# The first loads of a hybrid flow-matching layer: which queue issues them, and in which order the first projection's weights and the adaLN slabs follow

## The chip, the cores and the metric

One core of one Trainium2 chip runs the whole program. The metric is device time in microseconds (us) of one execution, lower is better; the profile shows one execution instruction by instruction. In the program's names PE is the matrix engine, DVE the vector engine, ACT the scalar engine, POOL the GpSimd engine and SP the engine that issues most transfers.

## The reference, cut to what matters

All 384 tokens (128 of a context, 256 latents) pass one layer. Only its first part bears on the change:

```python
mod = silu(cond) @ ada_w + ada_b                  # 6 x 2048 values for each of two condition vectors
h = rmsnorm(x, norm_w[0]) * (1 + scale_a) + shift_a
q, k, v, o, g, u = split(h @ w_in)                # each of q k v o u: 2048 -> 1024; g: 2048 -> 32
hm = mlstm_bidirectional(q, k, v, gates(g)) ; hp = pool_mixer(u)
x = x + gate_a * rmsnorm(concat(hm, hp) @ w_out, norm_w[1])
x = x + gate_f * rmsnorm(relu(h2 @ w1) ** 2 @ w2, norm_w[3])
```

## The kernel before

**Precision.** Every weight tile is loaded in float32 ("raw"), ACT copies it to a rounded `hi`, DVE subtracts to get `lo`, and each product is three matmuls: `hh*hi`, `hl*hi`, `hh*lo`, where `hh` and `hl` are the same split of the activations. `load_w` does one such tile: a transfer issued on SP, the ACT copy, the DVE subtraction. The raw tiles share 3 buffers, `hi` and `lo` have 4 each.

**The opening.** ACT's queue issues the condition vectors `cc` (two transfers), the constants `cst`, and four transfers of parameters into `prm`; SP issues the three tiles of x (1 MB each, `xtok`), then eight slabs of `ada_w` (512 KB each, `ada_raw`), then the first two weight tiles of u. POOL issues the gate bias, `mprev` and `n_in`. PE transposes the parameters (`pp`), then x (`xt`), and multiplies the slabs with silu of the condition vectors (`ada`). From that come the first columns of `mod`, and `make_h` makes the first `hm`, `hh`, `hl`.

**The u and v stage.** A loop of 8 steps `s` takes 256 rows of the contraction each. In a step five chunks pass: `("u", 0)`, `("u", 512)`, `("v", 0)`, `("v", 3)`, `("v", 6)`; the last also holds the gate columns. Each chunk is one weight tile and, on PE, 18 matmuls. Between the chunks stand the pieces of the adaLN product for the next step, `next(ada0)`: in a later step eight slabs are loaded (three after chunk 0, three after chunk 1, two after chunk 2), then 64 matmuls after chunk 2, the small transposing matmuls in the middle of chunk 3, and after it `make_h(s + 1)`. Four of the eight slabs use free halves of the tiles `u` and the tile `masks`, four the tiles `ada_raw`. The results of a chunk are added to SBUF tiles `u`, `v`, `gsb` by DVE (by ACT in step 0).

**What sets the order.** PE's order is the order of the code. On SP, DVE, ACT and POOL a scheduler places the instructions of this stage. Every engine works its list off in order, an instruction that waits holds up all behind it. Transfers issued by SP and ACT share 8 completion semaphores (`DMAHW0` to `DMAHW7`) handed out in turn; a transfer that takes a semaphore again first waits for the one that had it before. POOL's transfers have semaphores of their own (`DMASW`).

After this stage come pooling and the mLSTM, the output projection, and the MLP with most of the time.

Of the kernel before, what the change touches and what calls it, by code (L numbers as in the profile page):

```python
# [13 lines left out]
P = 128  # L14
# [11 lines left out]
N_CST = 15  # L26
# [9 lines left out]
RATE_GS = 0.25  # L36
S_FIRST, S_LAST, N_LAST = 1, 6, 2
LAG = 4
RATES = (1.5, 1.3, 1.3)
GATE_AT = 1, 6, 10  # L40

# [2 lines left out]
def hymba_kernel(  # L44
# [6 lines left out]
    nc = tc.nc  # L51
# [13 lines left out]
    def bank(name):  # L65
        return psum.tile([P, 512], F32, tag="ps", name=name)


    cst = const.tile([P, 3, P], F32, name="cst")
    cs_src = consts.rearrange("p (n q) -> p n q", q=P)  # L70
    ident = cst[:, C_ID, :]
    ones = cst[:, C_ONE, :]
    cc = const.tile([P, 2, 16], F32, name="cc")
# [2 lines left out]
    pre = pre_scope.enter_context(tc.tile_pool(name="pre", bufs=1))  # L76
    prm = pre.tile([P, 2, P], F32, name="prm")
    masks = vp.tile([P, N_CST - 3, P], F32, name="masks")
    nc.scalar.dma_start(cc[:, 0, :], c_ctx.rearrange("(p j) -> p j", j=16))
    nc.scalar.dma_start(cc[:, 1, :], c[0].rearrange("(p j) -> p j", j=16))  # L80
    nc.scalar.dma_start(cst[:, 0:3], cs_src[:, 0:3])

    vsb = [vp.tile([P, NH, 129], F32, name=f"v{i}") for i in range(3)]
    gsb = vp.tile([P, 3, 32], F32, name="gsb")
    x_tok = [pre.tile([P, D], F32, tag=f"x{i}", name=f"xtok{i}") for i in range(3)]
    for t, src in zip(x_tok, (x_prompt[0], x_sample[0, 0:128], x_sample[0, 128:256])):
        nc.sync.dma_start(t, src)
    nc.scalar.dma_start(prm[0:96, 1, :], ada_b[0].rearrange("(r p) -> r p", p=P))
    nc.scalar.dma_start(prm[0:64, 0, :], norm_w[0].rearrange("i (k p) -> (i k) p", p=P))
    nc.scalar.dma_start(prm[64:72, 0, :], mlstm_norm_w[0].rearrange("(k p) -> k p", p=P))  # L90
    nc.scalar.dma_start(prm[72:80, 0, :], pool_scale[0].rearrange("(k p) -> k p", p=P))
    gbias = const.tile([P, 32], F32, name="gbias")
    nc.gpsimd.dma_start(gbias, gate_bias[0].rearrange("g h -> (g h)").partition_broadcast(P))
    mprev = const.tile([40, 3], F32, name="mprev")
# [27 lines left out]
    def load_w(pieces, name, n=1024, after=(), later=None):  # L122

        raw = wp.tile([P, 1024], F32, tag="raw", name=f"raw_{name}", bufs=3)
        a = pieces[0][1].shape[1]
        rv = raw[:, 0:n].rearrange("p (a b) -> p a b", a=a)
        for off, src in pieces:
            load_w.ins = nc.sync.dma_start(rv[:, :, off:off + src.shape[2]], src).ins
        hi = wp.tile([P, 1024], F32R, tag="hi", name=f"hi_{name}", bufs=N_W)
        lo = wp.tile([P, 1024], F32R, tag="lo", name=f"lo_{name}", bufs=N_W)  # L130
        with ExitStack() as es:
            for ins in after:
                es.enter_context(tc.issue_after(ins))
            nc.scalar.activation(hi[:, 0:n], raw[:, 0:n], AF.Copy)  # L134
            low = lambda: nc.vector.tensor_tensor(lo[:, 0:n], raw[:, 0:n], hi[:, 0:n].bitcast(F32), op=ALU.subtract)  # L135
            if later is None:
                low()
            else:
                later.append(low)
        return (hi[:, 0:n].rearrange("p (a b) -> p a b", a=a), lo[:, 0:n].rearrange("p (a b) -> p a b", a=a))  # L140
# [27 lines left out]
    def gemm_T(w, cols, xs, n, evac, feeds=(), korder=(0, 1, 2, 3), name="g", hold=None):  # L168
# [3 lines left out]
        for g, c0 in enumerate(cols):  # L172
            for o in range(2):
                acc[g, o] = bank(f"acc_{name}_{c0}_{o}")
        beside = hold or (lambda ki, g: steps_done[-LAG] if len(steps_done) >= LAG else ())
        for ki, kc in enumerate(korder):
# [165 lines left out]
    NS = len(ksteps)  # L342
# [91 lines left out]
    chunks = [("u", 0, 512), ("u", 512, 512), ("v", 0, 3), ("v", 3, 3), ("v", 6, 2)]  # L434
# [17 lines left out]
    def load_chunk(s, ci, after=(), later=None):  # L452
        kind, c0, w = chunks[ci]
        ks = slice(ksteps[s][0], sum(ksteps[s]))
        if kind == "u":
            n, pieces = w, [(0, wv_in[:, ks, U0 + c0:U0 + c0 + w])]
        else:
            n, pieces = w * P, [(0, wv_in[:, ks, V0 + c0 * P:V0 + (c0 + w) * P])]
            if c0 == 6:
                pieces.append((n, wv_in[:, ks, 4 * M:4 * M + 32]))  # L460
                n += 32
        return load_w(pieces, f"{kind}_{c0}_{s}", ksteps[s][1] * n, after, later) + (n,)

    lo_later = []
    w_first = load_chunk(0, 0, later=lo_later)

    def shift_rows():
        for _ in range(2):
# [5 lines left out]
    h_ins = make_h(0, shift_rows)  # L474
# [6 lines left out]
    for s in range(NS):  # L481
        for ci, (kind, c0, w) in enumerate(chunks):
            k0, nk = ksteps[s]
            hi, lo, n = w_first if s == 0 and ci < 2 else load_chunk(s, ci, h_ins if s == 0 else ())
            if s == NS - 1 and ci == 4:
                with tc.issue_after(load_w.ins):
                    nc.sync.dma_start(masks, cs_src[:, 3:N_CST])
            acc = [bank(f"{kind}_{c0}_{s}_{i}") for i in range(3)]

            ways = ((0, 0), (1, 0), (0, 1))  # L490
            for ps in [ways[n:n + 1] for n in range(3)] if s == ci == 0 else [ways]:
                for k in range(nk):
                    for i in range(3):
                        for a, b in ps:
                            nc.tensor.matmul(acc[i][:, 0:n], h[k0 + k][a][:, i * P:(i + 1) * P], (hi, lo)[b][:, k, :],  # L495
                                             start=k == 0 and a + b == 0, stop=k == nk - 1 and b == 1)
                    if ci == 3 and k == 0:
                        next(ada0, None)
            if s == ci == 0:
                w_first = load_chunk(0, 1, h_ins)  # L500
            if s == 0 and ci == XT_AT:
                while len(xT) < KT:
                    transpose_x(len(xT))
            for _ in range((ADA_STEPS if s == 0 else (1, 1, 1, 0, 0))[ci]):
                next(ada0, None)
            if ci == 3 and s < NS - 1:
                make_h(s + 1)
            for i in range(3):
                if kind == "u":
                    dst, src = u_sb[i][:, c0:c0 + w], acc[i][:, 0:n]  # L510
                else:
                    dst, src = vsb[i][:, c0:c0 + w, 0:128], acc[i][:, 0:w * P].rearrange("p (h e) -> p h e", e=P)
                if s == 0:
                    nc.scalar.activation(dst, src, AF.Copy)
                else:
                    nc.vector.tensor_tensor(dst, src, dst, op=ALU.add)
                if kind == "v" and c0 == 6:
                    nc.vector.tensor_tensor(gsb[:, i, :], acc[i][:, w * P:n], gbias if s == 0 else gsb[:, i, :], op=ALU.add)
# [267 lines left out]
    def mid_vec():  # L786
        for i, q in ((4, 0), (4, 1), (3, 0), (3, 1), (2, 0)):
            yield from ada_vec(i, 1024 * q, 1024)

    ada2 = Feed(mid_vec(), RATES[0])  # L790

# [31 lines left out]

    ada2.rate = RATES[1]
    mixs = [None] * KT
# [35 lines left out]
    for k in range(8):  # L861
        mixs[k] = split_T(mix[k][:, 0:NTOK], f"mx{k}")
    ada2.rate = RATES[2]
    mo = [None] * KT
# [24 lines left out]
    for cols in ([0, 256], [512], [768], [1024], [1280], [1536], [1792]):  # L889
        if cols[0] in (768, 1024, 1280):  # L890
            for m in range(2):
                n = len(early)
# [496 lines left out]
```

## Time and profile before

| | before |
|---|---|
| median of 3 runs | 1690.18 us (1689.3 to 1690.31) |
| the profiled execution's own time | 1689.57 us |
| its span from first to last instruction | 1687.9 us |
| PE busy | 1656.9 us, 98% of the span |
| DVE busy | 1340.3 us, 79% |
| ACT busy | 752.4 us, 45% |
| POOL busy | 130.9 us, 8% |
| moved by DMA | 320.95 MB, mean 190 GB/s |

A row of the timeline or of the chain gives the start and the duration in us, then the engine, the line of the code and the operation. `SPq` and `ACTq` are the issuing of transfers. A bracket at the end of a row tells how long the engine was idle before, and what ended that. A row by stretches gives the busy time of the engines, the granted clock, the busy share of the DMA engines and GB/s.

### The profile page before, as it was taken

The numbers are of one execution on the slowest core, as the hardware profiler recorded it, in microseconds if no ns is written. First come the engines' busy times: TensorE is split into PE (matmuls) and PEld (weight loads), VectorE is DVE, ScalarE is ACT, GpSimd is POOL, SyncE is SP. The second block draws the span as 40 slices with busy tenths as digits, with TensorE's granted clock in tenths as the row PEclk, the third lists the DMA queues.
The fourth block names the chain that finished last, engine by engine and source line by source line (L and its number), as shares of the span: only waits on it lengthen the run. The fifth ranks groups of instructions, "written<-read, shape, count | busy, mean of one in ns | idle before, by whom it ended". The sixth has DMA issues, their size and how long they took to land.

```text
span 1687.9 us, 27859 instructions
## 1 busy us (share of the span) xinstructions
PE 1656.9 (98%) x10965; PEld 1582.5 (94%) x10965; DVE 1340.3 (79%) x2009; ACT 752.4 (45%) x1225; POOL 130.9 (8%) x181
## 2 busy tenths in 40 slices
PE   6999999999999999999999999999999999999997
PEld 4888999999999989989999999999999999999996
DVE  3677769898999959997797688988588488588688
ACT  4332355555443345543444444444444444444443
POOL 0000002221000024430000000000000000000120
PEclk9999999999999999999999999999999999999999
DMA  9999857777789964754546245544344443433653
GB/s 319 316 296 298 277 160 256 238 250 223 237 270 309 311 203 129 217 153 126 173 152 194 88 138 173 158 150 140 110 150 127 124 138 114 149 122 112 187 183 134
DMA packets 258195, 320.95 MB, mean 190 GB/s; under 512 B 14752, under 2 KB 223248, under 8 KB 257680
## 3 DMA queue, kind: packets, MB, share of 16 engines
q1 hardware_dynamic: 250256, 303.41, 57.0%
q0 software_dynamic: 5856, 13.69, 2.8%
q10 hardware_dynamic: 1952, 2.07, 0.4%
q8 instruction: 86, 1.41, 0.3%
q14 instruction: 45, 0.37, 0.1%
HBM read 308.61 MB, written 10.51 MB: 189 GB/s over the span
## 4 chain that ended last, share of the span: by engine, by line
PE 90%; DVE 4%; DMA 3%; issue 1%; SPq 1%; ACT 0%; POOL 0%; DVEq 0%; ACTq 0%; POOLq 0%
PE acc_w L144 10%; PE acc_w L143 10%; PE acc_w L145 10%; PE y L1223 4%; PE y L1224 4%; PE y L1222 4%; PE v L495 4%; PE u L495 3%; PE acc_wo L143 3%; PE acc_wo L144 3%; PE acc_wo L145 3%; PE y_yz L1223 2%; PE y_yz L1222 2%; PE y_yz L1224 2%; PE y L1066 2%; PE y L1065 2%
## 5 line engine op out<-in xcount | busy, mean ns | idle before, releaser
L144 PE MATMUL acc_w<-h2l,hi_w 128*128 128x384 f32 (+1 forms) x1024 | 346.2, 338 | 0.5 <-DVE h2l L1016 0.5
L143 PE MATMUL acc_w<-h2h,hi_w 128*128 128x384 f32 (+1 forms) x1024 | 344.2, 338 | 1.2 <-ACT h2h L1012 1.2
L145 PE MATMUL acc_w<-h2h,lo_w 128*128 128x384 f32 (+1 forms) x1024 | 345.1, 337 | 0.0
L135 DVE TENSOR_TENSOR lo_w<-raw_w,hi_w 128x1024 fp32r<-128x1024 f32 x152 | 185.3, 1221 | 137.0 <-ACT hi_w L134 136.8
L134 ACT ACTIVATE hi_w<-raw_w 128x1024 fp32r<-128x1024 f32 x152 | 160.8, 1058 | 215.2 <-PE acc_w L144 94.9
L316 DVE SCALAR_TENSOR_TENSOR ada_acc<-ada_raw,sg,ada_acc 128x1024 f32<-128x1024 f32 (+1 forms) x240 | 252.0, 1080 | 0.8 <-DMA ada_raw<-in_ada_w_dram 0.7
L143 PEld LDWEIGHTS acc_w<-h2h,hi_w 128*128 128x128 f32 x1024 | 192.2, 188 | 2.8 <-ACT h2h L1012 2.0
L144 PEld LDWEIGHTS acc_w<-h2l,hi_w 128*128 128x128 f32 x1024 | 192.6, 188 | 1.2 <-DVE h2l L1016 0.8
L145 PEld LDWEIGHTS acc_w<-h2h,lo_w 128*128 128x128 f32 x1024 | 192.4, 188 | 0.3 <-DVE lo_w L135 0.2
L1208 ACT ACTIVATE hi_t<-w 128x1024 fp32r<-128x1024 f32 x104 | 109.6, 1060 | 119.1 <-DVE w L1244 34.3
L1209 DVE TENSOR_TENSOR lo_t<-w,hi_t 128x1024 fp32r<-128x1024 f32 x104 | 126.3, 1220 | 15.1 <-ACT hi_t L1208 14.8
L1209 DVE TENSOR_TENSOR lo_b<-w,hi_b 128x1024 fp32r<-128x1024 f32 x78 | 95.3, 1221 | 41.9 <-ACT hi_b L1208 41.6
L1208 ACT ACTIVATE hi_b<-w 128x1024 fp32r<-128x1024 f32 x78 | 82.5, 1059 | 98.1 <-PE acc_w L144 66.7
L134 ACT ACTIVATE hi_wo<-raw_wo 128x1024 fp32r<-128x1024 f32 x32 | 34.0, 1064 | 80.6 <-DMA raw_wo<-in_w_out_dram 57.4
L942 ACT ACTIVATE z<-acc_w 128x384 f32<-128x384 f32 x54 | 26.3, 487 | 75.1 <-PE acc_w L145 75.1
L495 PE MATMUL v<-hi_v,hh 128*128 128x384 f32 (+1 forms) x144 | 48.0, 333 | 0.0
L134 ACT ACTIVATE hi_v<-raw_v 128x768 fp32r<-128x768 f32 (+1 forms) x24 | 19.0, 793 | 64.4 <-DMA raw_v<-in_w_in_dram 55.6
L495 PE MATMUL v<-lo_v,hh 128*128 128x384 f32 (+1 forms) x144 | 46.6, 324 | 1.0 <-DVE lo_v L135 1.0
L495 PE MATMUL v<-hi_v,hl 128*128 128x384 f32 (+1 forms) x144 | 46.5, 323 | 0.0
L135 DVE TENSOR_TENSOR lo_wo<-raw_wo,hi_wo 128x1024 fp32r<-128x1024 f32 x32 | 38.8, 1217 | 7.8 <-ACT hi_wo L134 7.0
L143 PE MATMUL acc_k<-hh,hi_k 128*128 128x384 f32 x128 | 44.2, 345 | 0.0
L143 PE MATMUL acc_o<-hh,hi_o 128*128 128x384 f32 x128 | 43.9, 343 | 0.0
(2264 smaller groups left out, 4549.0 us busy)
## 6 DMA issues: line engine op xcount, KB each, us to landing
raw_w<-in_w_dram SPq DMA_DIRECT2D x152, 512.0 KB, 4.2
ada_raw<-in_ada_w_dram SPq DMA_DIRECT2D x130, 512.0 KB, 4.7
w<-in_w_dram SPq DMA_DIRECT2D x104, 512.0 KB, 4.1
raw_wo<-in_w_out_dram SPq DMA_DIRECT2D x32, 512.0 KB, 5.1
u<-in_ada_w_dram SPq DMA_DIRECT2D x18, 512.0 KB, 6.6
raw_u<-in_w_in_dram SPq DMA_DIRECT2D x16, 512.0 KB, 7.0
raw_q<-in_w_in_dram SPq DMA_DIRECT2D x16, 512.0 KB, 4.8
raw_k<-in_w_in_dram SPq DMA_DIRECT2D x16, 512.0 KB, 4.9
```

What stands on the lines that cost most here:

```text
L134: nc.scalar.activation(hi[:, 0:n], raw[:, 0:n], AF.Copy)
L135: low = lambda: nc.vector.tensor_tensor(lo[:, 0:n], raw[:, 0:n], hi[:, 0:n].bitcast(F32), op=ALU.subtract)
L143: nc.tensor.matmul(ps, lh, rh, start=start, stop=False)
L144: nc.tensor.matmul(ps, lh, rl, start=False, stop=False)
L145: mm3.ins = nc.tensor.matmul(ps, ll, rh, start=False, stop=stop).ins
L316: nc.vector.scalar_tensor_tensor(acc[:, g, :], raw[:, a, :], cj, acc[:, g, :], op0=ALU.mult, op1=ALU.add)
L495: nc.tensor.matmul(acc[i][:, 0:n], h[k0 + k][a][:, i * P:(i + 1) * P], (hi, lo)[b][:, k, :], start=k == 0 and a + b == 0, stop=k == nk - 1 ...
L1208: nc.scalar.activation(hi, raw, AF.Copy)
L1209: nc.vector.tensor_tensor(lo, raw, hi.bitcast(F32), op=ALU.subtract)
L1222: nc.tensor.matmul(acc, xh, wh, start=start and j == 0, stop=False)
L1223: nc.tensor.matmul(acc, xh, wl, start=False, stop=False)
L1224: nc.tensor.matmul(acc, xl, wh, start=False, stop=stop and j == 3)
```

## The change

```diff
--- before.py
+++ after.py
@@ -36,6 +36,7 @@
 LAG = 4
+N_AHEAD = 3
 RATES = (1.5, 1.3, 1.3)
@@ -76,19 +77,19 @@
-    nc.scalar.dma_start(cc[:, 0, :], c_ctx.rearrange("(p j) -> p j", j=16))
-    nc.scalar.dma_start(cc[:, 1, :], c[0].rearrange("(p j) -> p j", j=16))
-    nc.scalar.dma_start(cst[:, 0:3], cs_src[:, 0:3])
+    nc.sync.dma_start(cc[:, 0, :], c_ctx.rearrange("(p j) -> p j", j=16))
+    nc.sync.dma_start(cc[:, 1, :], c[0].rearrange("(p j) -> p j", j=16))
+    nc.sync.dma_start(cst[:, 0:3], cs_src[:, 0:3])
...
     for t, src in zip(x_tok, (x_prompt[0], x_sample[0, 0:128], x_sample[0, 128:256])):
         nc.sync.dma_start(t, src)
-    nc.scalar.dma_start(prm[0:96, 1, :], ada_b[0].rearrange("(r p) -> r p", p=P))
-    nc.scalar.dma_start(prm[0:64, 0, :], norm_w[0].rearrange("i (k p) -> (i k) p", p=P))
-    nc.scalar.dma_start(prm[64:72, 0, :], mlstm_norm_w[0].rearrange("(k p) -> k p", p=P))
-    nc.scalar.dma_start(prm[72:80, 0, :], pool_scale[0].rearrange("(k p) -> k p", p=P))
+    nc.gpsimd.dma_start(prm[0:96, 1, :], ada_b[0].rearrange("(r p) -> r p", p=P))
+    nc.gpsimd.dma_start(prm[0:64, 0, :], norm_w[0].rearrange("i (k p) -> (i k) p", p=P))
+    nc.gpsimd.dma_start(prm[64:72, 0, :], mlstm_norm_w[0].rearrange("(k p) -> k p", p=P))
+    nc.gpsimd.dma_start(prm[72:80, 0, :], pool_scale[0].rearrange("(k p) -> k p", p=P))
@@ -462,7 +463,16 @@
-    w_first = load_chunk(0, 0, later=lo_later)
+    loaded = {0: load_chunk(0, 0, later=lo_later)}
+
+    def load_ahead(m, n):
+        for q in range(m, min(m + n, NS * len(chunks))):
+            if q not in loaded:
+                s, ci = divmod(q, len(chunks))
+                loaded[q] = load_chunk(s, ci, h_ins if s == 0 else ())
+                if q == NS * len(chunks) - 1:
+                    with tc.issue_after(load_w.ins):
+                        nc.sync.dma_start(masks, cs_src[:, 3:N_CST])
@@ -481,10 +491,8 @@
-            hi, lo, n = w_first if s == 0 and ci < 2 else load_chunk(s, ci, h_ins if s == 0 else ())
-            if s == NS - 1 and ci == 4:
-                with tc.issue_after(load_w.ins):
-                    nc.sync.dma_start(masks, cs_src[:, 3:N_CST])
+            load_ahead(5 * s + ci, 1 if s + ci == 0 else N_AHEAD)
+            hi, lo, n = loaded.pop(5 * s + ci)
@@ -497,7 +505,7 @@
             if s == ci == 0:
-                w_first = load_chunk(0, 1, h_ins)
+                load_ahead(1, 1)
```

The opening transfers change queues, and the loop asks for a chunk's weights two chunks before it uses them, ahead of the slabs that are asked for in between. PE's list stays as it was. POOL's list has the four parameter transfers more at its head, ACT's seven transfers fewer. On SP, DVE and ACT the order of this stage changes; behind it, it is the same.

The head of SP's list, before (`xtok` is x, `ada_raw` the first slabs; in brackets the semaphores that a transfer waits for):

```order
L87 DMA xtok_89<-in_x_prompt_dram 128x2048
L87 DMA xtok_90<-in_x_sample_dram 128x2048 [waits DMAHW0_49]
L87 DMA xtok_91<-in_x_sample_dram 128x2048 [waits DMAHW1_49]
L252 DMA ada_raw_0_0_146<-in_ada_w_dram 128x4x256 [waits DMAHW2_49]
L252 DMA ada_raw_0_4_158<-in_ada_w_dram 128x4x256 [waits DMAHW3_49]
L252 DMA ada_raw_0_8_170<-in_ada_w_dram 128x4x256 [waits DMAHW4_49]
```

The second tile of x waits for the semaphore of the first `cc` transfer, since ACT's seven and the first tile of x have used all eight. The same place in the list after the change:

```order
L80 DMA cc<-in_c_ctx_dram 128x16
L81 DMA cc<-in_c_dram 128x16
L82 DMA cst<-in_consts_dram 128x384
L88 DMA xtok_89<-in_x_prompt_dram 128x2048
L88 DMA xtok_90<-in_x_sample_dram 128x2048
L88 DMA xtok_91<-in_x_sample_dram 128x2048
L253 DMA ada_raw_0_0_146<-in_ada_w_dram 128x4x256
L253 DMA ada_raw_0_4_158<-in_ada_w_dram 128x4x256
L253 DMA ada_raw_0_8_170<-in_ada_w_dram 128x4x256 [waits DMAHW0_49]
```

Three small transfers now stand ahead of x, and the first wait stands at the third slab, five transfers later.

SP's list where step 1 is loaded, before (`raw_u_1` and `raw_v_1` are weights of step 1; `u`, `masks` and `ada_raw_4` are the eight slabs whose product is needed in step 1):

```order
L128 DMA raw_u_1_556<-in_w_in_dram 128x2x512
L365 DMA u_250<-in_ada_w_dram 128x4x256
L365 DMA u_251<-in_ada_w_dram 128x4x256
L365 DMA u_252<-in_ada_w_dram 128x4x256
L128 DMA raw_u_1_590<-in_w_in_dram 128x2x512
L365 DMA masks<-in_ada_w_dram 128x4x256
L365 DMA ada_raw_4_0_618<-in_ada_w_dram 128x4x256
L365 DMA ada_raw_4_4_620<-in_ada_w_dram 128x4x256
L128 DMA raw_v_1_625<-in_w_in_dram 128x2x384
L365 DMA ada_raw_4_8_652<-in_ada_w_dram 128x4x256
L365 DMA ada_raw_4_12_654<-in_ada_w_dram 128x4x256
L128 DMA raw_v_1_693<-in_w_in_dram 128x2x384
```

and after:

```order
L129 DMA raw_u_1_482<-in_w_in_dram 128x2x512
L129 DMA raw_u_1_535<-in_w_in_dram 128x2x512
L129 DMA raw_v_1_568<-in_w_in_dram 128x2x384
L366 DMA u_250<-in_ada_w_dram 128x4x256
L366 DMA u_251<-in_ada_w_dram 128x4x256
L366 DMA u_252<-in_ada_w_dram 128x4x256
L129 DMA raw_v_1_602<-in_w_in_dram 128x2x384
L366 DMA masks<-in_ada_w_dram 128x4x256
L366 DMA ada_raw_4_0_630<-in_ada_w_dram 128x4x256
L366 DMA ada_raw_4_4_632<-in_ada_w_dram 128x4x256
L129 DMA raw_v_1_637<-in_w_in_dram 128x2x256
```

The second u tile has moved ahead of three slabs, the first v tile ahead of six; the last two slabs now follow the last weight tile of the step.

DVE's list in step 1, before (`u<-u_1` adds a chunk's result, `lo` is the subtraction that makes a weight tile ready):

```order
L516 TENSOR_TENSOR u_250<-u_1_0_562,u_250 128x512
L135 TENSOR_TENSOR lo_u_1_593<-raw_u_1_590,hi_u_1_592 128x1024
L516 TENSOR_TENSOR u_251<-u_1_1_563,u_251 128x512
L516 TENSOR_TENSOR u_252<-u_1_2_564,u_252 128x512
L516 TENSOR_TENSOR u_250<-u_1_0_596,u_250 128x512
L516 TENSOR_TENSOR u_251<-u_1_1_597,u_251 128x512
L516 TENSOR_TENSOR u_252<-u_1_2_598,u_252 128x512
L135 TENSOR_TENSOR lo_v_1_628<-raw_v_1_625,hi_v_1_627 128x768
```

and after:

```order
L136 TENSOR_TENSOR lo_u_1_538<-raw_u_1_535,hi_u_1_537 128x1024
L449 SCALAR_TENSOR_TENSOR hl_521<-hm_519,mod,hh_520 128x256
L526 TENSOR_TENSOR gsb<-v_0_0_541,gbias 128x32
L526 TENSOR_TENSOR gsb<-v_0_1_542,gbias 128x32
L526 TENSOR_TENSOR gsb<-v_0_2_543,gbias 128x32
L136 TENSOR_TENSOR lo_v_1_571<-raw_v_1_568,hi_v_1_570 128x768
L524 TENSOR_TENSOR u_250<-u_1_0_574,u_250 128x512
L524 TENSOR_TENSOR u_251<-u_1_1_575,u_251 128x512
```

Both subtractions now stand ahead of the additions of the first u chunk.

ACT's list at the change from step 1 to step 2, before (`hi` rounds a weight tile, `hh` the next step's activations):

```order
L134 ACTIVATE hi_u_2_782<-raw_u_2_780 128x1024 [waits DMAHW6_49,DVE_49,PE_49]
L268 ACTIVATE ada_sb_4_688<-ada_583 128x256 [waits PE_49]
L447 ACTIVATE hh_726<-hm_725,mod 128x128 [waits DVE_49]
L447 ACTIVATE hh_726<-hm_725,mod 128x256 [waits DVE_49]
L447 ACTIVATE hh_731<-hm_730,mod 128x128 [waits DVE_49]
```

and after:

```order
L135 ACTIVATE hi_u_2_708<-raw_u_2_706 128x1024 [waits DVE_49,DMAHW2_49,PE_49,Activation_49]
L269 ACTIVATE ada_sb_4_701<-ada_595 128x256 [waits PE_49]
L135 ACTIVATE hi_u_2_761<-raw_u_2_759 128x1024 [waits DMAHW3_49,DVE_49]
L135 ACTIVATE hi_v_2_794<-raw_v_2_792 128x768 [waits DMAHW4_49,DVE_49,PE_49]
L448 ACTIVATE hh_739<-hm_738,mod 128x128 [waits DVE_49]
L448 ACTIVATE hh_739<-hm_738,mod 128x256 [waits DVE_49]
```

Two more roundings of weights, one of them waiting for PE and for a transfer, now stand ahead of the activations of the next step.

## The prediction

> **What bounds the kernel now.** I read the page first, then the chain of waits, then the waits of SP and PE, and last the DMA rates by short stretches in the opening. From the page:
>
> ```profile
> span 1687.9 us, 27859 instructions
> PE 1656.9 (98%) x10965; PEld 1582.5 (94%) x10965; DVE 1340.3 (79%) x2009; ACT 752.4 (45%) x1225; POOL 130.9 (8%) x181
> PE 90%; DVE 4%; DMA 3%; issue 1%; SPq 1%; ACT 0%; POOL 0%; DVEq 0%; ACTq 0%; POOLq 0%
> ```
>
> PE bounds the kernel. A gain can only be time in which PE stands still. The change touches the part up to the end of the u and v stage; behind it every engine's list is the same, so what PE gains by then should reach the end nearly whole. The chain of waits, in order of time (start, duration, what):
>
> ```profile
> 18.73 8.55 DMA raw_u<-in_w_in_dram
> ...
> 28.71 4.63 PE u L495 x18
> ...
> 52.21 2.79 PE u L495 x12
> 55.63 1.23 DVE lo_u L135
> ...
> 71.33 4.08 PE v L495 x27
> 75.41 8.38 PE u L495 x36
> ...
> 113.04 1.06 ACT hi_u L134
> ...
> 119.09 8.35 PE u L495 x36
> ...
> 140.36 8.34 PE u L495 x36
> ...
> 161.60 8.33 PE u L495 x36
> ...
> 182.85 8.36 PE u L495 x36
> ```
>
> The u rows from 52.21 on (the v row serves later) are the starts of steps 1, 2, 4, 5, 6 and 7. From step 4 to step 7 a step takes (182.85 - 119.09) / 3 = 21.25 us, and the chain is PE alone. Step 1 takes 75.41 - 52.21 = 23.20, which is 1.95 too many; steps 2 and 3 take 43.68 together, 1.18 too many. So there are three places to gain: the 28.7 us before the first u matmul, 1.95 in step 1, 1.18 in steps 2 and 3.
>
> **The opening.** SP's waits and the timeline:
>
> ```profile
> SPq L87 <- DMA cc<-in_c_ctx_dram: 4.8, 1, 4.8
> ...
> 0.80 0.42 ACTq L79 DMA_DIRECT2D cc<-in_c_ctx_dram  x1
> 0.81 0.38 SPq L87 DMA_DIRECT2D xtok<-in_x_prompt_dram  x1
> 6.01 0.81 SPq L87 DMA_DIRECT2D xtok<-in_x_sample_dram  x2
> 6.86 11.82 SPq L252 DMA_DIRECT2D ada_raw<-in_ada_w_dram  x8
> ...
> xtok<-in_x_prompt_dram SPq DMA_DIRECT2D x1, 1024.0 KB, 5.0
> ```
>
> SP stood 4.8 us until the first `cc` transfer had landed, only to take its semaphore again. The DMA rate by stretches of 1 us (last column GB/s) shows the price:
>
> ```profile
> 3.00:4.00 1.00, 0.00 (x0) 0.00 (x0) 0.00 (x0) 0.00 (x0) 0.71 (x5) 1.00 0.92 380
> 4.00:5.00 1.00, 0.00 (x0) 0.00 (x0) 0.00 (x0) 0.00 (x0) 0.00 (x0) 1.00 1.08 423
> 5.00:6.00 1.00, 0.00 (x0) 0.00 (x0) 0.00 (x0) 0.00 (x0) 0.00 (x0) 1.00 0.94 215
> 6.00:7.00 1.00, 0.00 (x0) 0.00 (x0) 0.04 (x1) 0.71 (x1) 0.00 (x0) 1.00 0.76 162
> 7.00:8.00 1.00, 0.39 (x1) 0.18 (x1) 0.31 (x2) 0.99 (x3) 0.00 (x0) 1.00 0.75 123
> 8.00:9.00 1.00, 0.58 (x2) 0.28 (x2) 0.90 (x6) 0.97 (x3) 0.00 (x0) 1.00 0.94 385
> ...
> 29.00:30.00 1.00, 1.00 (x5) 0.69 (x5) 0.95 (x4) 1.00 (x4) 0.00 (x0) 1.00 1.07 342
> ...
> 61.00:62.00 1.00, 0.53 (x2) 0.20 (x2) 1.00 (x2) 0.00 (x0) 0.00 (x0) 1.00 0.50 149
> ```
>
> From 8 us the DMA engines are full (the row at 29 us is one of many like it; the first deep dip behind it that matters is at 61 us, last row), and the first u matmul hangs on the landing of `raw_u` (the chain above), so the opening is bound by bytes. A transfer issued at 6.01 is at full rate at about 8.0, 1.9 us later. After the change x stands behind three small transfers. SP takes about 0.43 us for one (0.81 for two, and gaps), so x's first tile is issued at 0.81 + 3 * 0.43 = 2.1, not 0.81, and flows from 4.0. Its 1.05 MB (1024 KB) at 0.40 MB/us, between the rows at 3 and 4 us, take 2.6 us, to 6.6; for the constants and parameters among it I add 0.4. The second tile then flows from about 7.0 without a gap, where before it flowed from 8.0. I take 0.9 us. Bounds: 1.3 lost, if the dead stretch stays and only the three issues count; 1.7 won, if the whole shortfall of 5 to 8 us goes (3 * 390 - 500 = 670 KB at 390 GB/s) and the issues cost nothing.
>
> The Trainium skill ("DMA: Bandwidth & Descriptors", section "Issuing engines are not separate DMA queues") says that all issuing engines feed the same 16 DMA engines, and that issuing from several at once only saves issue time. By that the opening would lose the three issues, 1.3 us, instead of winning 0.9. No row here contradicts the sharing; but the SP row shows a wait of 4.8 us which that rule does not count, so I go by the row.
>
> The parameters on POOL cost nothing. A POOL issue and its landing:
>
> ```profile
> 1.33 0.70 POOL L93 DMA_DIRECT2D gbias<-in_gate_bias_dram  x1 [0.81 <-POOLq L1376]
> gbias<-in_gate_bias_dram POOLq DMA_DIRECT2D x1, 16.0 KB, 5.2
> ...
> 13.90 0.47 PE L402 MATMUL xt<-cst,xtok 128*128 128x128 f32 x1 [2.10 <-DMA xtok<-in_x_sample_dram]
> ```
>
> Four issues of 0.70 from 1.33 on end at 4.1; the last lands at 3.43 + 5.2 = 8.6. PE needs them for `pp`, then waits for x's third tile until 13.90 anyway: that is the cover, 5 us of it, and without it the cost would be some 0.3 us. `gbias`, `mprev`, `n_in` go out 2.8 us later and are used after 50 us. ACT, rid of seven issues, waits for `cc` as before. The masks' transfer in step 7 has until pooling, past 190 us; nothing.
>
> **Step 1.** What PE waited for, and the rows that made it late:
>
> ```profile
> PEld v L495 <- DVE lo_v L135: 1.3, 1, 1.3
> PEld u L495 <- DVE lo_u L135: 0.5, 1, 0.5
> ...
> 55.02 0.69 DVE L516 TENSOR_TENSOR u<-u,u 128x512 f32<-128x512 f32 x1 [2.01 <-PE u L495]
> ...
> 60.01 0.85 ACT L134 ACTIVATE hi_v<-raw_v 128x768 fp32r<-128x768 f32 x1 [5.38 <-DMA raw_v<-in_w_in_dram]
> 61.54 0.95 DVE L135 TENSOR_TENSOR lo_v<-raw_v,hi_v 128x768 fp32r<-128x768 f32 x1
> ...
> 65.61 3.59 PE ada L372 x64
> ```
>
> The second `lo_u` stood on DVE behind an addition that waited for PE, and `raw_v` landed at 60.0, with six slabs ahead of it in a full DMA. After the change these six come behind it: 3.1 MB, 9 us at 350 GB/s (an estimate from the row at 29 us), so it lands near 51, and its subtraction stands ahead of the additions. Both waits go. What is late next are the slabs for step 1, but the bytes up to the last of them are the same that flowed by 61 us before; less the 0.9 they land about 62, with an estimated 2 from bytes to semaphore, and PE wants the first at 65.6 - 1.9 - 0.9 = 62.8, the last two only after 48 of the 64 matmuls, 2.7 later. I take the whole 1.95; bounds 0 and 1.95.
>
> **Steps 2 and 3.** The 1.18 went where two `hi_u`, the later waiting for a transfer until 113.04, stood on ACT ahead of `ada_sb`. After the change those two weights are asked for a chunk or two earlier and land, by the same count, some 4 us ahead of need. I take 1.18; bounds: all of it, and a loss as in the third rival.
>
> **Sum.** 0.9 + 1.95 + 1.18 = 4.0 us. The profiled execution took 1689.57 us, 1.7 over its span and 0.6 under the median 1690.18; it would take 1685.5, and the median becomes 1686.2.
>
> **Rivals.** The margins of the new order, from steps 2 and 3 of before:
>
> ```profile
> 72.85 1.60 ACT L447 ACTIVATE hh<-hm,mod 128x128 fp32r<-128x128 f32 x4 [3.20 <-DVE hm L442]
> 77.33 1.21 DVE L135 TENSOR_TENSOR lo_u<-raw_u,hi_u 128x1024 fp32r<-128x1024 f32 x1
> 86.95 3.59 PE ada L372 x64
> ```
>
> *The opening gives nothing.* The gap stays, because the first transfers are slow whatever their queue, and x is three issues late: from -1.3 to +0.2, and with the stalls gone 1686.9 to 1688.4. It is the mechanism that would follow from the rule above; 0.5 MB in three poor microseconds, part of them spent on small packets, speaks for it, the 4.8 us wait against it. Chance 0.2.
>
> *The slabs become the late ones.* In step 2 the last two slabs are queued behind a v tile whose buffer comes free with the second `lo_u`, at 78.5 before, 75.7 with the gains. Then 1.34 MB (3.8 us at 350 GB/s), 1.9 to start and about 2 to land give 83.4; PE's slab product starts at 86.95 - 2.85 = 84.1 and needs these two at its end, 2.7 later. It holds by 3 us; each us that SP or the queue is later eats it. If half of the stalls come back, or step 1 wins half: 1687.2 to 1689.6. Chance 0.15.
>
> *Slower.* On ACT `hh` now stands behind `hi_v` of the next step, whose buffer PE frees at the end of chunk 3: 9 of the 27 matmuls (the wider ones) into the v row of 71.33, about 73.1, or 70.25 with the gains of 2.85. With 0.85 for `hi_v` that moves `hh` from 72.85 - 2.85 = 70.0 to 71.1, and PE wants the first pair at 75.41 - 2.85 = 72.6: 0.6 us to spare after two of 0.4. If the v tile's transfer lands more than 0.6 us after its buffer is free, PE waits by the rest, at each of six step changes. It decides for slower than before where that rest is over 4.0 / 6 = 0.7 us; over 1.2 it is past 0.2%. With 1.5 the time is 1690.2 + 9 - 4 = 1695. Against it: in step 6 of before, `hh` already stood behind a `hi_v`, and from 161.60 to 182.85 it took the plain 21.25. Chance 0.05.
>
> *No change*, the scheduler's waits put back what is won: 1690 within 0.5, chance 0.04.
>
> **How the numbers follow.** The forecast has 0.56, from 1685.0 to 1687.0. A measurement of this kernel tells about 0.2%, 3.4 us, so faster is under 1686.8: nearly all of the forecast, 0.54. Slower by over 0.2%: 0.05. The rest, 0.41, is within 0.2%. The range from 1684.9 to 1688.9 leaves out the end of the slab rival, no change and slower, and a little below.
>
> **What would show it.** Right: SP's first x issue near 2.1 and the next two right behind, no wait at L88; full DMA rate without a dip from 4 us; the first u matmul near 27.8; steps of 21.25 us from step 1 on, PE without a wait for `lo_u` or `lo_v`; step 7 starting near 178.8. Wrong: the first u matmul at 28.7 or later; waits of PE for slabs (L373) or for `hh` (L448); ACT's `hi_v` ahead of `hh` ended by a transfer; or a gain by 183 us that is lost behind it.

## The result, and the profile after

The changed kernel takes 1685.13 us (median of 10; 1684.09 to 1686.67) against 1689.28 (median of 10) of the kernel before on the same chip: 0.9979 of its time, 95% interval 0.997 to 0.9987 (the ratios here are those on record; they are not the quotients of two medians). A second set, later, gave 0.9989 (0.998 to 0.9998). So it is faster by one or two thousandths, on the edge of what such a measurement can tell. The forecast was 1686.2, and 1685.13 lies in its range. That it is so near is partly luck: the loop won what was worked out for it, the opening lost where it was to win.

The page of the profiled execution (1684.17 us):

```profile
span 1682.5 us, 27870 instructions
PE 1654.3 (98%) x10965; PEld 1581.4 (94%) x10965; DVE 1340.3 (80%) x2009; ACT 751.3 (45%) x1225; POOL 133.3 (8%) x185
```

The chain of waits after (start, duration, what), the stage that the change touches:

```profile
3.61 12.58 DMA ada_raw<-in_ada_w_dram
...
29.84 4.61 PE u L503 x18
...
53.21 8.32 PE u L503 x36
...
74.48 8.38 PE u L503 x36
...
117.06 8.35 PE u L503 x36
...
180.82 8.36 PE u L503 x36
```

Step 1 takes 74.48 - 53.21 = 21.27 us (23.20 before), steps 2 and 3 take 42.58 (43.68 before), and there is no more `lo_u`, `lo_v` or `hi_u` in the chain. But the first u matmul starts at 29.84, 1.13 later than before. Step 7 starts at 180.82, 2.03 earlier.

The opening after, by SP's rows, by stretches (the last three columns are the granted clock, the busy share of the DMA engines and GB/s), and by PE's rows (in brackets the idle time before a row and what ended it):

```profile
2.18 0.43 SPq L88 DMA_DIRECT2D xtok<-in_x_prompt_dram  x1
2.65 0.91 SPq L88 DMA_DIRECT2D xtok<-in_x_sample_dram  x2
3.61 15.66 SPq L253 DMA_DIRECT2D ada_raw<-in_ada_w_dram  x8
```

```profile
8.00:9.00 1.00, 0.14 (x1) 0.17 (x2) 0.00 (x0) 0.97 (x3) 0.00 (x0) 1.00 1.70 213
9.00:10.00 1.00, 0.44 (x2) 0.12 (x2) 0.41 (x2) 1.00 (x2) 0.00 (x0) 1.00 0.46 156
10.00:11.00 1.00, 0.00 (x0) 0.00 (x0) 0.00 (x0) 0.01 (x1) 0.00 (x0) 1.00 0.88 330
```

```profile
14.73 0.47 PE L403 MATMUL xt<-cst,xtok 128*128 128x128 f32 x1 [1.98 <-DMA xtok<-in_x_sample_dram]
16.32 1.08 PE L257 MATMUL ada<-ada_raw,cT 128*32 128x256 f32 x8 [1.11 <-DMA ada_raw<-in_ada_w_dram]
```

SP's wait is gone and x is issued as worked out, at 2.18 to 3.56. The dead stretch did not go, it moved: from 5 to 8 us to 8 to 11 (400 GB/s just ahead of it, 405 behind). x's third tile comes at 14.73 instead of 13.90. The busy share counts the whole time of a packet in the row in which it starts, so 1.70 stands for packets that run on into the next row.

All kernels of this study in one table. "Slab product" is the start of the first `ada` matmul on PE, "first u" and "step 7" the starts of those u matmuls (us):

| kernel | slab product | first u | step 7 | first u to step 7 | ratio to before (95%) |
|---|---|---|---|---|---|
| before | 15.54 | 28.71 | 182.85 | 154.1 | |
| before, again (b2) | 15.45 | 28.62 | 183.17 | 154.6 | 1.0002 (0.9993 to 1.0011) |
| after | 16.32 | 29.84 | 180.82 | 151.0 | 0.9979 (0.997 to 0.9987) |
| after, again (a2) | 17.78 | 30.99 | 182.01 | 151.0 | 0.9989 (0.998 to 0.9998) |
| new opening, old loop (e1) | 16.11 | 29.30 | 183.54 | 154.2 | 1.0012 (1.0003 to 1.0021) |
| old opening, new loop (e2) | 15.19 | 28.94 | 179.94 | 151.0 | 0.9981 (0.9972 to 0.999) |
| after, parameters on ACT (e3) | 16.85 | 30.35 | 181.32 | 151.0 | 0.9986 (0.9977 to 0.9994) |
| after, constants on ACT (e4) | 15.29 | 28.45 | 179.43 | 151.0 | 0.9978 (0.9969 to 0.9987) |
| after, nothing on POOL (f1) | 14.55 | 27.73 | 178.75 | 151.0 | 0.997 (0.9959 to 0.9981) |
| f1 again (f1b) | 14.29 | 27.47 | 178.61 | 151.1 | 0.9974 (0.9966 to 0.9983) |
| f1, x's first tile first (f2) | 14.21 | 28.66 | 180.21 | 151.6 | 0.9972 (0.9962 to 0.9982) |
| f1's opening, old loop (f3) | 14.89 | 28.08 | 182.92 | 154.8 | 1.0001 (0.9992 to 1.001) |
| before, nothing on POOL (g2) | 15.32 | 28.54 | 184.56 | 156.0 | 1.0007 (0.9998 to 1.0016) |
| after, one chunk ahead (n2) | 16.88 | 30.05 | 181.02 | 151.0 | 0.9983 (0.9974 to 0.9992) |

### The profile page after: what moved, and what is told of

Same layout as the page of the kernel before. It is cut to its first block, busy times and chain, and to the rows that moved or that the text cites. A ratio compares the mean times of both kernels' runs of the same rounds, so it can differ in the third digit from the quotient of the medians.

```text
span 1682.5 us, 27870 instructions
## 1 busy us (share of the span) xinstructions
PE 1654.3 (98%) x10965; PEld 1581.4 (94%) x10965; DVE 1340.3 (80%) x2009; ACT 751.3 (45%) x1225; POOL 133.3 (8%) x185
## 4 chain that ended last, share of the span: by engine, by line
PE 94%; DVE 3%; issue 1%; DMA 1%; ACT 0%; SPq 0%; POOL 0%; DVEq 0%; ACTq 0%; POOLq 0%
PE acc_w L145 10%; PE acc_w L144 10%; PE acc_w L146 10%; PE v L503 4%; PE y L1231 4%; PE y L1232 4%; PE y L1230 4%; PE u L503 4%; PE acc_wo L144 3%; PE acc_wo L145 3%; PE acc_wo L146 2%; PE y_yz L1231 2%; PE y_yz L1230 2%; PE y_yz L1232 2%; PE y L1074 2%; PE y L1073 2%
```

## The experiments

### Each part of the change alone

e1 has the new opening and the loop of before, e2 the old opening and the new loop:

```diff
 # e1: before.py with
-    nc.scalar.dma_start(cc[:, 0, :], ...)      # and cc[:, 1], cst
+    nc.sync.dma_start(cc[:, 0, :], ...)
-    nc.scalar.dma_start(prm[0:96, 1, :], ...)  # and three more
+    nc.gpsimd.dma_start(prm[0:96, 1, :], ...)
 # e2: before.py with N_AHEAD, load_ahead and its two calls
```

> The new opening with the old loop. Theory A (the new opening by itself costs what the changed kernel shows there, 1.1 us at the first u matmul, and the loop's part is separate): first u matmul near 29.8 us, steps 1 to 3 lose their 1.95 and 1.18 us as before, step 7 starts near 184.0, time 1.1 us over before (ratio 1.0007). Rival B (the later opening in the changed kernel's profile is chance, or comes from the loop's order): first u matmul near 28.7, ratio 1.000.

> The new loop with the old opening. Theory A: first u matmul near 28.7 us, every step from 1 on takes 21.3 us, step 7 starts near 179.7, time 3.1 us under before (ratio 0.9981), 1 us better than the change as a whole. Rival B (the loop needs the new opening's lead or its semaphores): waits of PE for lo_u or lo_v stay in step 1, gain under 2 us.

The chain of e1:

```profile
29.30 4.61 PE u L495 x18
...
52.71 2.79 PE u L495 x12
...
75.90 8.38 PE u L495 x36
```

and of e2:

```profile
28.94 4.62 PE u L503 x18
...
52.33 8.32 PE u L503 x36
...
73.60 8.38 PE u L503 x36
```

In e1 step 1 takes 23.19 as before, in e2 21.27. The opening alone makes the first u matmul 0.6 later (theory A had 1.1, rival B none) and the time longer, 1.0012; the loop alone makes step 7 start 2.91 earlier and gives 0.9981, as theory A had it. In the new loop the stretch from the first u to step 7 is 151.0 or 151.1 us whatever the opening (151.6 in f2 alone); in the old one 154.1 or more. So the loop term of the sum is shown, with its size, and the sign of the opening term was wrong.

### Where the opening lost

Two first guesses. e3 puts the four parameter transfers back on ACT's queue, so that POOL issues as little as before; e4 puts `cc` and `cst` back on ACT, so that x is SP's first transfer without the wait:

```diff
 # e3: after.py with
-    nc.gpsimd.dma_start(prm[0:96, 1, :], ...)   # and three more
+    nc.scalar.dma_start(prm[0:96, 1, :], ...)
 # e4: after.py with
-    nc.sync.dma_start(cc[:, 0, :], ...)         # and cc[:, 1], cst
+    nc.scalar.dma_start(cc[:, 0, :], ...)
```

> The changed kernel with the four parameter transfers issued by ACT instead of POOL; condition vectors and constants stay ahead of x on SP. Theory A (the dip of the DMA rate at 8 to 10 us in the changed kernel is the parameters' software packets, up to 1.9 us each on a DMA engine, in the middle of x): no such dip, first u matmul near 28.8, 1 us earlier than in the changed kernel. Rival C (all of the opening's loss is x standing behind three issues; the dip comes anyway): first u matmul stays near 29.8.

> The changed kernel with the condition vectors and constants issued by ACT again, so that x is first on SP; parameters stay on POOL. Both theories let x flow 1.3 us earlier. Theory A: the dip by software packets stays, first u matmul near 28.5 us. Rival C (the whole loss is the three issues): first u matmul near 28.4 with no dip left; if x's first bytes are no earlier, the start of a transfer is not bound by its issue.

e3's first u matmul came at 30.35, later than any theory had it. There is no dip at 8 to 10 us any more, but one at 3 to 5:

```profile
3.00:4.00 1.00, 0.00 (x0) 0.00 (x0) 0.00 (x0) 0.62 (x1) 0.71 (x5) 1.00 0.74 137
4.00:5.00 1.00, 0.00 (x0) 0.00 (x0) 0.00 (x0) 0.89 (x2) 0.00 (x0) 1.00 1.00 141
```

x's first tile took 8.0 us from issue to landing, 5.5 in after: `gbias`, `mprev` and `n_in` now leave POOL earlier and meet its start (58 packets, 16.4% of the DMA engines from 2 to 6 us). What share the four transfers on ACT had in it was not separated. e4's chain:

```profile
1.73 12.30 DMA cst<-in_consts_dram
...
28.45 4.62 PE u L503 x18
```

`cst`, 192 KB, needed 12.3 us to land, since now no pause of SP lets it through: PE stood at `pp` until 14.2. And the dip at 9 us was there as well (112 GB/s from 9 to 10 us). So neither the parameters alone nor the place of x explains the dip.

What was left was the rest of POOL's queue. All packets from 8 to 10 us after, and the queues (packets, MB, share of the time of 16 DMA engines):

```profile
DMA packets 94, 0.37 MB, mean 184 GB/s; under 512 B 34, under 2 KB 51, under 8 KB 51
q0 software_dynamic: 47, 0.02, 57.6%
q1 hardware_dynamic: 47, 0.35, 50.4%
```

47 packets of POOL's queue with 0.02 MB in all take more of the DMA engines' time than 0.35 MB of x: 0.576 * 2 us * 16 / 47 = 0.39 us each on average. That average hides two kinds. Read packet by packet from the trace, 30 of the 47 have 4 bytes and take 0.009 us; the other 17 take 1.07 us on average, up to 1.96, and nearly all of them have 1 KB. POOL's queue has just 16 packets of 1 KB in the opening: these 16 KB are `gbias`, the one transfer of that size on it, which gives every partition the same 128 bytes. They start at 7.99 to 8.92 us, after POOL issued `gbias` at 3.61, and take 18.2 us of engine time together, 1.1 us of all 16 engines. The parameters' large packets, 32 of 2 and 3 KB from 2.7 to 4.0 us, take 8.6.

The dips lie where `gbias` is: its packets start at 2.8 to 4.6 us in e3, at 8.0 to 9.3 in e4. Before, POOL issued it at 1.33, and its packets started at 5.0 to 5.5 and took 5.4 us together. So what the change did on POOL's queue was to push `gbias` behind four issues, into the middle of x.

f1 has no transfer on POOL's queue in the opening:

```diff
 # f1: after.py with
-    nc.gpsimd.dma_start(prm[0:96, 1, :], ...)   # and three more
+    nc.sync.dma_start(prm[0:96, 1, :], ...)     # behind x
-    nc.gpsimd.dma_start(gbias, ...)             # and mprev, n_in
+    nc.sync.dma_start(gbias, ...)               # behind u's first weight tile
```

> The changed kernel, with the parameters, gbias, mprev and n_in issued by SP behind x instead of by POOL's queue, so that no transfer of POOL's queue is under way while x flows; every value is computed. The question is why the changed opening ends 0.6 to 1.1 us later than before although x was issued earlier. Theory A: the slow packets of POOL's queue (0.56 to 0.69 us on average, up to 1.95, between 8 and 10 us of the changed kernel) hold up the x tiles behind them on the same DMA engines. Then the DMA rate has no dip below 350 GB/s between 5 and 11 us, x's third tile lands near 13.0 to 13.5 instead of 14.7, the first u matmul starts near 28.0 instead of 29.84, and the time is about 1683.4. Theory B: the dip comes from so many large transfers in a row whatever stands beside them; then it stays, the third tile lands at 14.5 or later, the first u matmul starts at 29.5 to 30, and the time stays at 1685.1 within 1.

The same queues and stretches of f1:

```profile
q1 hardware_dynamic: 119, 0.84, 101.0%
```

```profile
8.00:9.00 1.00, 0.00 (x0) 0.00 (x0) 0.00 (x0) 0.97 (x3) 0.00 (x0) 1.00 1.04 434
9.00:10.00 1.00, 0.00 (x0) 0.00 (x0) 0.00 (x0) 0.81 (x3) 0.00 (x0) 1.00 0.98 410
10.00:11.00 1.00, 0.00 (x0) 0.00 (x0) 0.00 (x0) 1.00 (x2) 0.00 (x0) 1.00 0.98 410
```

```profile
12.99 0.39 PE L376 MATMUL pp<-cst,prm 96*128 96x96 f32 x1 [12.99 <-DMA prm<-in_ada_b_dram]
...
14.55 1.08 PE L254 MATMUL ada<-ada_raw,cT 128*32 128x256 f32 x8
```

0.84 MB flow in the two microseconds in which 0.37 flowed, the dip is gone, and the first u matmul starts at 27.73, the slab product at 14.55. Theory A (28.0) was right, B (29.5 to 30) fell; the time, 1684.51, is 1.1 above what A had, and the average of POOL's packets is the 0.39 above, not 0.56 to 0.69. A second profile (f1b) has 27.47. The parameters, now behind x in SP's queue, hold PE until 12.99; that costs at most 0.1, for the first slab lands at 14.42. Issued by SP, `gbias` went as 128 packets of 128 bytes that take 0.013 us each, beside a full stream at 25 us. f1 takes all of POOL's transfers away; a run that moves `gbias` alone wasn't made, so its share is read from the packets, and why its packets are so slow on POOL's queue isn't shown.

f2 issues x's first tile ahead of `cc` and `cst` in f1:

```diff
+    nc.sync.dma_start(x_tok[0], x_prompt[0])
     nc.sync.dma_start(cc[:, 0, :], ...)
     ...
-    for t, src in zip(x_tok, ...):
+    for t, src in zip(x_tok[1:], ...):
```

> As the run before it, with x's first tile issued ahead of cc and cst on SP; every value is computed. Theory A: the opening is bound by bytes, and the first tile now flows 1.3 us earlier (issue at 0.81 instead of 2.1), so the first u matmul starts near 26.8 to 27.3 and the time is near 1682.3. Theory B: packets of different queues alternate, so the 64-byte packets of cc and cst stand between x's 8 KB packets, land only with x's first tile near 6 to 7 us, and the transposes and the chain from cc to the first u matmul start no earlier than in the run before: the first u matmul within 0.4 of that run's, and the time too.

Its first u came at 28.66, which neither theory had. The slab product began earlier than in f1, 14.21, so the transfers are no reason. Rows of PE in f2:

```profile
14.21 1.08 PE L255 MATMUL ada<-ada_raw,cT 128*32 128x256 f32 x8 [0.36 <-DMA ada_raw<-in_ada_w_dram]
...
19.75 1.08 PE L255 MATMUL ada<-ada_raw,cT 128*32 128x256 f32 x8
...
21.91 0.64 PE L255 MATMUL ada<-ada_raw,cT 128*32 128x256 f32 x8
```

and in f1:

```profile
16.40 1.08 PE L254 MATMUL ada<-ada_raw,cT 128*32 128x256 f32 x8
18.00 0.64 PE L254 MATMUL ada<-ada_raw,cT 128*32 128x256 f32 x8
```

The same eight matmuls take 1.08 us at first and 0.64 later. In f2 four groups were slow, in f1 two, in `after` three; it lasts 2 to 7 us from the slab product on. It ends where the trace's record of the granted clock begins, with the full clock: at 20.74 us in f2, 17.68 in f1, 20.83 in `after`. In all 14 profiles single matmuls of these groups take 0.60 to 0.64 us when they end before that moment, and 0.38 to 0.41 when they start behind it. For the time before its record begins the column of the granted clock has 1.00, so it doesn't show this. So f2's full clock came 3.1 us later than f1's, and its first u with it. From the slab product to the first u that makes 13.2 to 14.5 us, so in the table "slab product" tells the transfers' share better than "first u": of the 1.13 us that `after` is late, 0.78 are there already. By the time f2 and f1 can't be told apart.

### The opening of before, and the opening without the loop

g2 takes POOL's transfers out of the opening of before; f3 has f1's opening with the loop of before:

```diff
 # g2: before.py with
-    nc.gpsimd.dma_start(gbias, ...)             # and mprev, n_in
+    nc.sync.dma_start(gbias, ...)               # behind u's first weight tile
 # f3: g2 with
-    nc.scalar.dma_start(cc[:, 0, :], ...)       # and cc[:, 1], cst, four of prm
+    nc.sync.dma_start(cc[:, 0, :], ...)
```

> The kernel before, with gbias, mprev and n_in issued by SP behind u's first weight tile instead of by POOL's queue in the opening; everything is computed. The question is what made the poor stretch of 5 to 8 us (123 to 215 GB/s). Theory A (the prediction): SP's wait of 4.8 us for cc's semaphore, which delays x's second and third tiles to 6.0; then the stretch stays as it was within 60 GB/s, x's third tile lands at 13.4 to 13.9, the first u matmul starts at 28.3 to 28.8, and the time is 1688.7 within 0.8. Theory B: the slow packets of POOL's queue (0.6 us each at 4 to 6 us); then the second tile flows without the stretch, the third lands by 12.9, the first u matmul starts by 27.9, and the time falls by about 0.9.

> The opening of the run without transfers on POOL's queue (cc, cst, x and the parameters issued by SP, then gbias, mprev, n_in later), with the loop of the kernel before (weights behind the slabs); everything is computed. Theory A: x issued without the wait is worth what the prediction said, about 0.9 to 1.0 us, once no transfer of POOL's queue stands beside it: first u matmul at 27.6 to 28.0 against 28.7, step 1 still about 23.2, steps 2 and 3 together still about 43.7 to 43.9, step 7 at 181.7 to 182.2, time 1687.7 to 1688.0. Theory B: the gain of the opening is lost again in step 1, whose slabs and weights hang on bytes and not on PE; then step 7 starts at 182.6 or later and the time is as before within 0.3.

g2's stretches:

```profile
5.00:6.00 1.00, 0.00 (x0) 0.00 (x0) 0.00 (x0) 0.00 (x0) 0.00 (x0) 1.00 0.97 307
6.00:7.00 1.00, 0.04 (x1) 0.07 (x1) 0.20 (x1) 0.57 (x1) 0.00 (x0) 1.00 0.09 23
7.00:8.00 1.00, 0.79 (x3) 0.40 (x3) 0.01 (x1) 0.99 (x3) 0.00 (x0) 1.00 1.02 180
```

The three rows move 510 KB, those of before 500 (215, 162 and 123): the hole is as deep without POOL's transfers, now with idle DMA engines in its middle (0.09), and the third tile comes at 13.73. Not every row stayed within the 60 GB/s of theory A, but the sum and the arrival did, and B fell: before, the hole was SP's wait, as the prediction read it; after, it is `gbias` on POOL's queue. (The 0.6 us each in theory B was the longest packet; the average of the 1 KB packets of before is 0.33.)

The loop of g2 lost, though: its first u came at 28.54, 0.2 earlier than before, and its step 7 at 184.56, 1.7 later. The time is 1.0007, 1689.58, just above what A had. Its chain has, in step 0:

```profile
37.20 8.27 DMA raw_v<-in_w_in_dram
```

f3's chain:

```profile
27.14 9.29 DMA raw_v<-in_w_in_dram
...
36.76 7.89 DMA raw_v<-in_w_in_dram
...
52.45 2.81 PE u L495 x12
...
75.60 8.39 PE u L495 x36
```

Its first u came at 28.08, 0.6 earlier than before, its step 7 where it was before, and the time is 1.0001. Theory B has the number, but not the place: step 1 takes 23.15 as ever, and the gain is lost already in step 0, whose chain is transfers of v's weights: 24.4 us instead of 23.5. g2, whose opening is hardly earlier, takes 24.7 there, with two such rows in its chain. Both have three small transfers more on SP behind u's first weight tile, and in both SP issues v's second weight tile behind four slabs, at 36.8 us or later; in before it goes out ahead of these, by 31.9. That order may be what took f3's gain, so whether an earlier opening is worth anything in the old loop as it was isn't shown; one that is 0.6 later (e1) made step 7 0.7 later. In the new loop an earlier opening counts whole (151.0 from the first u to step 7 in f1 too).

### How much lead the loop needs

n2 asks one chunk ahead instead of two:

```diff
-N_AHEAD = 3
+N_AHEAD = 2
```

> The changed kernel with N_AHEAD = 2 instead of 3: the weights are asked for one chunk ahead instead of two; the opening is the changed one. Theory A (the prediction's working): step 1 lost 1.95 us because raw_v stood behind six slabs; one chunk ahead puts raw_v of step 1 ahead of the last pair of slabs only or of none of them, so a part of step 1's loss comes back, 0.5 to 1.95 us: step 1 takes 21.8 to 23.2, steps 2 and 3 22.0 to 22.5 where the late hi_u comes back too; the time is 1686 to 1688. Theory B: any lead of a chunk is enough; all steps take 21.25 to 21.3, and the time is 1685.1 within 0.8.

```profile
53.42 8.32 PE u L503 x36
...
74.68 8.38 PE u L503 x36
```

Step 1 takes 21.26 and first u to step 7 again 151.0: theory B was right, one chunk is enough (the time, 1685.96, is 0.1 above its range). SP's rows in step 1 of n2:

```profile
39.90 1.83 SPq L129 DMA_DIRECT2D raw_u<-in_w_in_dram  x2
41.78 4.18 SPq L366 DMA_DIRECT2D u<-in_ada_w_dram  x3
48.48 0.37 SPq L129 DMA_DIRECT2D raw_v<-in_w_in_dram  x1
```

Already with this lead both u tiles stand ahead of all slabs and `raw_v` behind three of them instead of six.

### What two sets of one kernel differ by

> The kernel before, unchanged, timed against itself: what two sets of runs of one kernel differ by, and which parts of its trace recur. Theory A: the steps of the u and v stage start at the same times within 0.1 us (28.7, 52.05, 75.25, 96.56, 118.9), so the differences of the stage belong to the change, and the time is 1.000 within 0.1%; the drop of the granted clock at 541 to 545 us, which the profiles of different kernels show for 0, 3.4 or 6.8 us, comes at random. Theory B: the opening itself varies by about 1 us from one execution to the next (x's third tile landing between 13.5 and 15), so the 1.1 us by which the changed opening is later is no property of the change.

> The changed kernel a second time, unchanged. The stage that the change touches ended 2.04 us earlier in its profile, and the median of the time was 4.15 lower, with an interval from 2.2 to 5.1 by the ratio. Theory A: the stage's 2.0 us (3.0 in the loop less 1.0 in the opening) is all there is, and the rest of the first difference came by chance: the ratio is 0.9983 to 0.9991, and the profile may or may not show the drop of the granted clock near 545 us. Theory B: the change is worth 4 us, by something behind the stage; the ratio is 0.9970 to 0.9980, and the stretch from step 7 to the end is again shorter than the 1503.7 to 1505.2 of the kernel before.

> The changed kernel without transfers of POOL's queue in the opening, a second time and beside the changed kernel itself, to set the two against each other on one chip; everything is computed. Theory A: it beats the changed kernel by the 2.1 us that its first u matmul is earlier: first u 27.7, step 7 at 178.6, time 1.5 to 2.5 us under the changed kernel's of this set. Theory B: that is lost behind the stage: within 0.8 us of the changed kernel.

The kernel before against itself gives 1.0002, and its stage starts within 0.1 us up to 96.6, then within 0.4. For the opening of before theory A was right, then. The changed opening varies by about 1 us, as theory B had it: in a2 PE's first slab product waited until 17.78, first u 30.99. From 2 to 10 us a2 moved no less than `after` (2.31 MB against 2.23), and x's first tile landed 1.8 later all the same; why isn't shown. The queues of a2 from 8 to 10 us:

```profile
q1 hardware_dynamic: 68, 0.48, 66.2%
q0 software_dynamic: 70, 0.01, 36.6%
```

Its ratio, 0.9989 (0.998 to 0.9998), is what theory A expected of it. f1b, run beside it, took 1684.14 against 1685.90; the means of 11 times each are 1684.34 and 1686.46, a ratio of 0.9987 (0.9980 to 0.9994, by drawing anew from the two sets). Theory A was right for it: f1 is faster than both kernels, by about what its opening ends earlier (2.1 us by the first profiles).

## Why the prediction was right, and where not

**The opening: the term that failed.** It was +0.9 us with bounds of -1.3 and +1.7. Measured by the first u matmul: -1.1 (after), -2.3 (a2), -1.3 (n2), -0.6 (e1); the prediction's own sign of being wrong, a first u at 28.7 or later, came. The issue times came as worked out (2.18, then in a row; no wait at L88), and so did x's first bytes. The step that failed is the passage that the parameters on POOL cost nothing: it counted POOL's issues and when the last lands (8.6 worked out; PE got it at 8.86), took PE's wait for them as the whole price, and let `gbias` go out later at no price because it is used late. It went out 2.3 us later (2.8 was worked out), and its 16 packets took 18.2 us of the DMA engines' time while x flowed, where they had taken 5.4 before. Taking the parameters alone off POOL doesn't help: in e3, with these on ACT and `gbias` at x's start, the slab product is later still, 16.85. Without transfers on POOL's queue, in f1, f1b and f3, PE's slab product starts at 14.29 to 14.89 against 15.19 to 15.54 with the opening of before: 0.8 us on average, close to the 0.9. So x without the wait is worth about what was worked out for it.

**The rule that was weighed against it.** The prediction set a loss of the three issues, 1.3 us, against its gain. A loss came, but f1 has the same three issues ahead of x and gains, so the issues are not what it lost. By the Trainium skill ("DMA: Bandwidth & Descriptors", section "Issuing engines are not separate DMA queues") the transfers of all issuing engines run on the same 16 DMA engines; the queue rows show that at work between POOL's and SP's. The same page of the Trainium skill (section "Queues, rings and completion order") says that each of these engines takes turns between its queues, packet by packet. e4 agrees with that: from 4 to 8 us 197 packets went on ACT's queue and 197 on SP's.

**Steps 1, 2 and 3: right in place and size.** 1.95 was expected of step 1, 1.93 measured; 1.18 of steps 2 and 3, 1.10 measured; every wait named there is gone from PE's list, and e2 shows them alone. The slabs did not become late (no wait at L373), `hh` never held PE up behind `hi_v` (six steps of 21.24 to 21.31 us), so the third and second rivals did not come about. The likeliest rival, an opening that gives nothing, did: by the first u matmul it came near the lower end of its range in after and beyond it in a2. Its time, 1686.9 to 1688.4, did not come, nor its reason, that the first transfers are slow whatever their queue: in f1 they aren't.

**The sum, and the end.** 3.0 in the loop and 0.1 in step 0, less 1.1 in the opening, make 2.0 at step 7, half of the 4.0 forecast. The profiled execution was 1689.57 - 1684.17 = 5.4 us shorter all the same; 3.4 of that lie behind the stage, which the prediction held to be unchanged; that they brought the time near the forecast is luck. Half of it is the clock. Rows of before and, in the second fence, of after:

```profile
542.00:544.00 2.00, 1.36 (x11) 1.36 (x12) 2.00 (x6) 1.35 (x3) 0.00 (x0) 1.00 1.06 378
544.00:546.00 2.00, 2.00 (x9) 2.00 (x9) 2.00 (x6) 0.20 (x1) 0.00 (x0) 0.64 1.06 383
546.00:548.00 2.00, 2.00 (x8) 2.00 (x8) 1.91 (x2) 1.23 (x5) 0.00 (x0) 0.51 1.08 350
```

```profile
538.00:540.00 2.00, 1.42 (x12) 1.33 (x10) 2.00 (x3) 1.35 (x3) 0.00 (x0) 1.00 1.07 375
540.00:542.00 2.00, 1.83 (x13) 1.83 (x14) 2.00 (x6) 0.88 (x3) 0.00 (x0) 1.00 1.08 376
```

PE has the same short stop in both (1.36 and 1.42 us busy of 2), 0.75 us from the end of one matmul to the start of the next. In before the granted clock then falls to a half for 3.4 us, which costs 1.7; in after it doesn't. Of the 14 profiles of this study 7 show 3.4 us of it, e4 shows 6.8, and 6 none; old and new loops are on both sides.

What decides it can be read from the traces. In every profile the changes of the granted clock lie whole multiples of 3.413 us apart (in before 525.66 us = 154 of them, from the start of the record to the fall). All 14 have the same stop of 0.75 us. Where it began 0.7 to 2.2 us into such a window, the clock fell (8 profiles); where it began 2.7 to 3.2 or 0.1 to 0.2 into one, it didn't (6). Where the windows lie differs from execution to execution of one kernel (the first record is at 17.68 in f1 and 16.60 in f1b), so this part is luck and not the change. The Trainium skill ("TensorE: Matmul & The Clock Gate", section "What's actually happening") says that the clock is set by the activity in a window of about 3.4 us that runs freely. The traces agree, by these multiples.

The rest of the 3.4 lies in waits for DVE's results (`lo_t` and `lo_b` of a later stage: 2.4 us in before, 1.1 in after) and in smaller ones, which differ between two profiles of one kernel too: `lo_t` and `lo_b` took 1.8 in f1 and 1.0 in f1b, and from step 7 to the end b2 is 1.5 us shorter than before. The profiles tie 2.0 us to the change in the first set and 1.2 (a2 against b2) in the last; the times gave 4.15 and 2.8 by the medians, 3.5 and 1.9 by the ratios, each with an interval of some 1.5 us to both sides. Whether another microsecond was won behind the stage stays open: from step 7 to the end the five profiles of old loops average 1503.8 us and the nine of new ones 1503.4, less apart than two profiles of one kernel.

## What to carry to other kernels

Moving loads off the path of other loads is worth what the stalls in the chain say, and a lead of one chunk was enough for it. Moving small loads to another queue is not free because PE doesn't wait for them: ask what else flows through the DMA engines at that time, and what the move does to the transfers that stand behind them in that queue; here it was one of these that cost. Behind the large ones on the same queue they cost nothing in the new loop (f1), but in the old one v's second weight tile came out behind four slabs, and step 0 took 0.9 to 1.2 us longer (f3, g2): read the whole list again. And a change of 1 or 2 us in the opening can be the clock's doing: compare the first product, not what comes behind it.

## What the hardware showed that was not expected

- A small transfer on POOL's queue can stall a full stream: the 16 packets of 1 KB of `gbias`, which gives all partitions the same 128 bytes, took 0.05 to 1.96 us each in after, 1.1 on average, more than three times an 8 KB packet of x (0.31 in f1 at that time). On SP's queue the same 16 KB went as 128 packets of 0.013 us.
- A queue with small transfers starves beside one with large ones: `cst` (192 KB) took 12.3 us in e4 and 2.6 in after, where it stood ahead of x on the same queue. Before, its packets flowed from 5.3 to 6.3 us, when x's first tile had passed and SP stood still.
- PE's first groups of eight matmuls take 1.08 us instead of 0.64, for 2 to 7 us, at different lengths in otherwise equal openings, until the record of the granted clock begins; the column shows 1.00 for the time before, too.
- A stop of PE of 0.75 us was enough to halve the granted clock for 3.4 us (1.7 us lost), in the 8 of 14 profiles in which it began 0.7 to 2.2 us into one of the clock's windows of 3.413 us (6.8 us in one of them, e4).
